# RMSNorm with SiLU on one core: block 0's first row leaves in a transfer of its own

## The chip, the cores and the metric

The kernel runs on one core of a Trainium2 chip. The metric is the device time of one execution in microseconds (us), as the median of several runs. The engines that matter are VectorE (DVE), ScalarE (ACT), which also issues stores to its DMA queue, SyncE (SP), which issues loads to its own, and the core's 16 DMA engines, which carry the packets of both queues. TensorE (PE) is used only at the start.

## What is computed

The input `x` has 8 x 1024 rows of 2048 float32 values, 67.1 MB; the output has the same size. Each row is divided by its root mean square, multiplied by `gamma`, and put through SiLU:

```python
rms = np.sqrt(np.mean(x ** 2, axis=-1, keepdims=True) + eps)
out = gamma * x / rms
return (out * (1 / (1 + np.exp(-out)))).astype(np.float32)
```

## The kernel before

The 8192 rows are cut into 16 blocks of 512. A block is a tile `xt` of 128 partitions; each partition holds J = 4 neighbouring rows, 32 KB that are contiguous in DRAM, so a block is one load of 4 MB (line 52) and, but for the last, one store of 4 MB (line 93). Six buffers hold the blocks. Before anything else one of them serves as `grow`, into which gamma is loaded (line 108); PE copies gamma to all partitions (line 112).

The work of a block `b` has three parts, and all of it happens in place:

- `sums(b)`, lines 58 to 75: the sums of squares. DVE takes rows 2 and 3 (line 64), ACT rows 0 and 1 (line 68, Square with an accumulator); ACT then takes the square root (line 74).
- `invert(b)`, line 79: DVE's reciprocal.
- `finish(b)`, lines 82 to 90: for each of the four rows DVE multiplies by the reciprocal and by gamma (line 84). After rows 1 and 3 ACT applies SiLU to the pair of rows just done (line 88). With `halves`, for the last block alone, the pair is stored at once (line 90).

The order on each engine is the order in which the program is written, since the kernel uses a manual schedule. Loads 0 to 4 are issued at the start, load 5 once `grow` is free. Then block 0 is summed, inverted and finished, block 1 is summed, and from there the loop of lines 124 to 127 runs `sums(b + 1, after_first=[b - 1])`, `finish(b)`, `invert(b + 1)`. The argument `after_first` is where stores are issued: `sums` calls `store(b - 1)` after its first Square (lines 70 to 72), so block 0's store is issued by ACT in the middle of `sums(2)`. `store(b)` also issues load `b + 6` on SP (line 95). That load writes into the buffer that block `b` leaves, so SP waits until the store has landed. The last stores are issued by lines 128, 130 and 90.

The DMA issues of ACT stand in ACT's instruction order, those of SP in SP's. Each transfer is spread over the 16 DMA engines, 8 partitions on each, one packet per partition; a small packet at the end of each engine's share updates a semaphore.

Of the kernel before, what the change touches and what calls it, by code (L numbers as in the profile page):

```python
# [1 line left out]

# [4 lines left out]

ACT = mybir.ActivationFunctionType
ALU = mybir.AluOpType


@with_exitstack
def kernel(
    ctx: ExitStack,
    tc: tile.TileContext,
    x: bass.AP,
    gamma: bass.AP,
    eps: bass.AP,
    out: bass.AP,
):  # L20

    nc = tc.nc
    P = nc.NUM_PARTITIONS
    f32 = mybir.dt.float32
    x2 = x.flatten_outer_dims()
    o2 = out.flatten_outer_dims()  # L30
    n, d = x2.shape
    J = 4
    BUFS, LEAD = 6, 6
    nblk = n // (P * J)
    xb = x2.rearrange("(b p j) d -> b p (j d)", p=P, j=J)
    ob = o2.rearrange("(b p j) d -> b p (j d)", p=P, j=J)

    singles = ctx.enter_context(tc.tile_pool(name="singles", bufs=1))
    pool = ctx.enter_context(tc.tile_pool(name="pool", bufs=BUFS))
    small = ctx.enter_context(tc.tile_pool(name="small", bufs=2))  # L40
    psum = ctx.enter_context(tc.tile_pool(name="psum", bufs=1, space=bass.MemoryType.PSUM))

    g = singles.tile([P, d], f32)
    eps_t = singles.tile([P, 1], f32)
    ones = singles.tile([P, P], f32)
    junk_a = psum.tile([P, d], f32, name="junk_a")
    junk_v = psum.tile([P, d], f32, name="junk_v")
    blocks, rmss, rstds = {}, {}, {}

    def load(b):  # L50
        xt = pool.tile([P, J * d], f32, name="xt")
        nc.sync.dma_start(out=xt, in_=xb[b])  # L52
        blocks[b] = xt

    def row(b, j):
        return blocks[b][:, j * d:(j + 1) * d]

    def sums(b, after_first=()):


        ss = small.tile([P, J], f32, name="ss")
        na = J // 2
        for j in range(na, J):
            nc.vector.tensor_tensor_reduce(  # L64
                out=junk_v, in0=row(b, j), in1=row(b, j), scale=1.0, scalar=0.0,
                op0=ALU.mult, op1=ALU.add, accum_out=ss[:, j:j + 1])
        for j in range(na):
            nc.scalar.activation(out=junk_a, in_=row(b, j), func=ACT.Square,  # L68
                                 accum_out=ss[:, j:j + 1])
            if j == 0:  # L70
                for s in after_first:
                    store(s)
        rms = small.tile([P, J], f32, name="rms")
        nc.scalar.activation(out=rms, in_=ss, func=ACT.Sqrt, scale=1.0 / d, bias=eps_t)  # L74
        rmss[b] = rms

    def invert(b):
        rstd = small.tile([P, J], f32, name="rstd")
        nc.vector.reciprocal(out=rstd, in_=rmss.pop(b))  # L79
        rstds[b] = rstd  # L80

    def finish(b, halves=False):
        for j in range(J):
            nc.vector.scalar_tensor_tensor(out=row(b, j), in0=row(b, j), scalar=rstds[b][:, j:j + 1],  # L84
                                           in1=g, op0=ALU.mult, op1=ALU.mult)
            if j % 2:
                cols = slice((j - 1) * d, (j + 1) * d)
                nc.scalar.activation(out=blocks[b][:, cols], in_=blocks[b][:, cols], func=ACT.Silu)  # L88
                if halves:
                    nc.scalar.dma_start(out=ob[b][:, cols], in_=blocks[b][:, cols])  # L90

    def store(b):
        nc.scalar.dma_start(out=ob[b], in_=blocks[b])  # L93
        if b + LEAD < nblk:
            load(b + LEAD)

    with tc.manual_schedule():


        Q = 4  # L100
        w = d // Q
        grow = pool.tile([P, J * d], f32, name="xt")
        for b in range(BUFS - 1):
            load(b)
        nc.vector.memset(ones, 1.0)  # L105
        nc.vector.memset(eps_t, float(eps))  # L106
        nc.scalar.activation(out=junk_a[:, 0:1], in_=ones[:, 0:1], func=ACT.Square)  # L107
        nc.scalar.dma_start(out=grow[0:P:P // Q, 0:w],
                            in_=bass.AP(tensor=gamma.tensor, offset=gamma.offset, ap=[[w, Q], [1, w]]))
        for c in range(Q):  # L110
            k = c * (P // Q)
            nc.tensor.matmul(junk_v[:, c * w:(c + 1) * w], ones[k:k + 1, :], grow[k:k + 1, 0:w],  # L112
                             start=True, stop=True)
        nc.vector.tensor_copy(out=g, in_=junk_v)  # L114
        load(BUFS - 1)


        last = nblk - 1
        sums(0)
        invert(0)  # L120
        finish(0)
        sums(1)
        invert(1)
        for b in range(1, last - 1):
            sums(b + 1, after_first=[b - 1])
            finish(b)
            invert(b + 1)
        store(last - 2)
        finish(last - 1)
        store(last - 1)  # L130
        sums(last)
        invert(last)
        finish(last, halves=True)


# [1 line left out]
_INS = ['x', 'gamma', 'eps']  # L137
_OUTS = [((8, 1024, 2048), 'float32')]

_NUMBERS = {'eps': 9.999999747378752e-06}  # L140


# [26 lines left out]
```

## Time and profile before

| | us |
|---|---|
| Median of 4 runs (317.46 to 317.84) | 317.72 |
| The profiled execution | 317.7 |
| Its span, from first to last instruction | 315.9 |
| DVE busy | 223.5 (71% of the span) |
| ACT busy | 223.8 (71%) |
| PE busy | 2.1 (1%) |
| One 4 MB load, issue to landing (median of 16) | 41.5 |
| One 4 MB store, issue to landing (median of 15) | 35.8 |
| One 2 MB store of the last block, the same (median of 2) | 10.6 |

The DMA engines moved 134.25 MB, 425 GB/s over the span. "Busy" is time in which an engine executes instructions; DMA issues aren't counted in it. Issue to landing includes the time that a transfer stands in its queue behind others, so a large figure alone doesn't say that the transfer is slow. In the rows of stretches, the columns are: the stretch in us from the start of the span, its length, the busy time of PE, PE's weight load, DVE, ACT and GpSimd with their instruction counts, the granted PE clock, the mean busy share of the 16 DMA engines, and GB/s. A packet is counted where its record lies, so a short stretch can show a share over 1.

### The profile page before, as it was taken

The numbers are of one execution on the slowest core, as the hardware profiler recorded it, in microseconds if no ns is written. First come the engines' busy times: TensorE is split into PE (matmuls) and PEld (weight loads), VectorE is DVE, ScalarE is ACT, GpSimd is POOL, SyncE is SP. The second block draws the span as 40 slices with busy tenths as digits, with TensorE's granted clock in tenths as the row PEclk, the third lists the DMA queues.
The fourth block names the chain that finished last, engine by engine and source line by source line (L and its number), as shares of the span: only waits on it lengthen the run. The fifth ranks groups of instructions, "written<-read, shape, count | busy, mean of one in ns | idle before, by whom it ended". The sixth has DMA issues, their size and how long they took to land.

```text
span 315.9 us, 444 instructions
## 1 busy us (share of the span) xinstructions
PE 2.1 (1%) x8; PEld 0.5 (0%) x8; DVE 223.5 (71%) x147; ACT 223.8 (71%) x144; POOL 0.2 (0%) x4
## 2 busy tenths in 40 slices
PE   0200000000000000000000000000000000000000
PEld 0000000000000000000000000000000000000000
DVE  0679499999494884939759296693957939993900
ACT  1357958999967778668777677676686776889440
POOL 0000000000000000000000000000000000000000
DMA  8999999999999999999999999999999999999996
GB/s 333 402 461 415 448 386 411 456 407 465 398 462 402 457 411 452 419 444 431 431 436 431 444 419 448 415 456 407 461 402 461 407 456 407 456 411 452 427 420 290
DMA packets 4763, 134.25 MB, mean 425 GB/s; under 512 B 532, under 2 KB 532, under 8 KB 536
## 3 DMA queue, kind: packets, MB, share of 16 engines
q1 hardware_dynamic: 2304, 67.11, 49.8%
q10 hardware_dynamic: 2456, 67.12, 49.2%
q14 instruction: 3, 0.02, 0.0%
HBM read 67.12 MB, written 67.11 MB: 425 GB/s over the span
## 4 chain that ended last, share of the span: by engine, by line
DMA 66%; DVE 18%; ACT 8%; issue 4%; DVEq 1%; ACTq 0%; SPq 0%
DMA xt<-in_x_dram 44%; DMA out_dram<-xt 23%; DVE xt L84 13%; ACT xt L88 5%; DVE junk_v L64 4%; ACT junk_a L68 2%; ACT L74 1%; DVEq L164 1%; ACT rms L74 0%; DVE rstd L79 0%; DVE ss L64 0%; ACTq L93 0%; SPq L52 0%; DVEq L64 0%; ACTq L74 0%
## 5 line engine op out<-in xcount | busy, mean ns | idle before, releaser
L84 DVE SCALAR_TENSOR_TENSOR xt<-xt,rstd,g 128x2048 f32<-128x2048 f32 x64 | 146.2, 2348 | 0.1
L88 ACT ACTIVATE xt<-xt 128x4096 f32<-128x4096 f32 x32 | 115.4, 3615 | 36.8 <-DVE xt L84 36.7
L64 DVE CUSTOM_DVE_ANT_0 junk_v<-xt 128x2048 f32<-128x2048 f32 x32 | 73.6, 2298 | 55.5 <-DMA xt<-in_x_dram 54.9
L68 ACT ACTIVATE junk_a<-xt 128x2048 f32<-128x2048 f32 x32 | 60.1, 1879 | 28.6 <-DMA xt<-in_x_dram 27.7
L74 ACT ACT_TABLE_LOAD x15 | 19.2, 1283 | 9.9 <-DVE ss L64 9.9
L88 ACT ACT_TABLE_LOAD x15 | 19.2, 1283 | 3.1 <-DVE xt L84 2.9
L79 DVE RECIPROCAL rstd<-rms 128x4 f32<-128x4 f32 x16 | 2.8, 174 | 11.3 <-ACT rms L74 11.3
L114 DVE COPY g<-junk_v 128x2048 f32<-128x2048 f32 x1 | 2.3, 2292 | 9.3 <-PE junk_v L112 9.3
L68 ACT ACTIVATION_READ_ACCUMULATOR junk_a<-xt 128x1 f32 x32 | 6.0, 186 | 0.0
L74 ACT ACTIVATE rms<-ss,eps_t 128x4 f32<-128x4 f32 x16 | 4.8, 297 | 1.2 <-DVE ss L64 1.1
L64 DVE DVE_READ_ACCUMULATOR2_ANT ss<- 128x1 f32 x32 | 4.5, 142 | 0.0
L112 PE MATMUL junk_v<-xt,ones 1*128 1x512 f32 x8 | 2.1, 1132 | 8.1 <-DMA xt<-in_gamma_dram 8.1
L107 ACT ACT_TABLE_LOAD x1 | 1.3, 1283 | 0.7 <-PEq L150 0.7
L105 DVE MEMSET ones<- 128x128 f32 x1 | 0.2, 165 | 0.8 <-PEq L150 0.8
L112 PEld LDWEIGHTS junk_v<-xt,ones 1*128 1x128 f32 x8 | 0.5, 308 | 8.1 <-issue 8.1
L107 ACT ACTIVATE junk_a<-ones 128x1 f32<-128x1 f32 x1 | 0.2, 174 | 0.0
L150 POOL MEMSET const-uint8-127<- 128x1 uint8 x1 | 0.1, 102 | 0.0
L150 POOL MEMSET const-bfloat16-1.0<- 128x1 bf16 x1 | 0.1, 101 | 0.0
L150 POOL MEMSET const-float32-0.0<- 128x1 f32 x1 | 0.1, 98 | 0.2 <-issue 0.2
L150 POOL MEMSET const-float32-1.0<- 128x1 f32 x1 | 0.1, 98 | 0.0
L106 DVE MEMSET eps_t<- 128x1 f32 x1 | 0.1, 59 | 0.0
## 6 DMA issues: line engine op xcount, KB each, us to landing
xt<-in_x_dram SPq DMA_DIRECT2D x16, 4096.0 KB, 41.5
out_dram<-xt ACTq DMA_DIRECT2D x15, 4096.0 KB, 35.8
out_dram<-xt ACTq DMA_DIRECT2D x2, 2048.0 KB, 10.6
xt<-in_gamma_dram ACTq DMA_DIRECT2D x1, 8.0 KB
```

Of the source, the lines that this page charges most:

```text
L64: nc.vector.tensor_tensor_reduce(out=junk_v, in0=row(b, j), in1=row(b, j), scale=1.0, scalar=0.0, op0=ALU.mult, op1=ALU.add, accum_out=ss[ ...
L68: nc.scalar.activation(out=junk_a, in_=row(b, j), func=ACT.Square, accum_out=ss[:, j:j + 1])
L74: nc.scalar.activation(out=rms, in_=ss, func=ACT.Sqrt, scale=1.0 / d, bias=eps_t)
L79: nc.vector.reciprocal(out=rstd, in_=rmss.pop(b))
L84: nc.vector.scalar_tensor_tensor(out=row(b, j), in0=row(b, j), scalar=rstds[b][:, j:j + 1], in1=g, op0=ALU.mult, op1=ALU.mult)
L88: nc.scalar.activation(out=blocks[b][:, cols], in_=blocks[b][:, cols], func=ACT.Silu)
L105: nc.vector.memset(ones, 1.0)
L107: nc.scalar.activation(out=junk_a[:, 0:1], in_=ones[:, 0:1], func=ACT.Square)
L112: nc.tensor.matmul(junk_v[:, c * w:(c + 1) * w], ones[k:k + 1, :], grow[k:k + 1, 0:w], start=True, stop=True)
L114: nc.vector.tensor_copy(out=g, in_=junk_v)
L150: nc = _bacc.Bacc("TRN2", target_bir_lowering=False, num_devices=1)
L164: with _tile.TileContext(nc) as tc:
```

## The change

Block 0's store is cut in two. In `finish(0)`, right after the SiLU of rows 0 and 1, ACT issues a store of row 0 alone: 8 KB in each partition, 1 MB. The other three rows, 24 KB in each partition, 3 MB, are stored where the whole block was stored, after the first Square of `sums(2)`. Row 1 is done when row 0 is, but goes with the later transfer. Load 6, which takes block 0's buffer, is issued at the same place in SP's order. All other blocks are stored as they were.

```diff
             if j == 0:
                 for s in after_first:
-                    store(s)
+                    store(s, slice(0 if s else 1, J))
...
-    def finish(b, halves=False):
+    def finish(b, halves=False, first_row=False):
...
                 nc.scalar.activation(out=blocks[b][:, cols], in_=blocks[b][:, cols], func=ACT.Silu)
+                if first_row and j == 1:
+                    nc.scalar.dma_start(out=ob[b][:, 0:d], in_=row(b, 0))
                 if halves:
                     nc.scalar.dma_start(out=ob[b][:, cols], in_=blocks[b][:, cols])
 
-    def store(b):
-        nc.scalar.dma_start(out=ob[b], in_=blocks[b])
+    def store(b, rows=slice(0, J)):
+        c = slice(rows.start * d, rows.stop * d)
+        nc.scalar.dma_start(out=ob[b][:, c], in_=blocks[b][:, c])
         if b + LEAD < nblk:
             load(b + LEAD)
...
-        finish(0)
+        finish(0, first_row=True)
```

## The prediction

> **What bounds the kernel now.** I read the page's slices and queues first, then the DMA rate in stretches, the chain that ended last, and the timeline around the edit. The page's slices and queue rows:
>
> ```profile
> DMA  8999999999999999999999999999999999999996
> GB/s 333 402 461 415 448 386 411 456 407 465 398 462 402 457 411 452 419 444 431 431 436 431 444 419 448 415 456 407 461 402 461 407 456 407 456 411 452 427 420 290
> q1 hardware_dynamic: 2304, 67.11, 49.8%
> q10 hardware_dynamic: 2456, 67.12, 49.2%
> ```
>
> All slices but the two end ones have the 16 DMA engines at 90% or more, and the packets of loads (q1) and stores (q10) together fill 99.0% of 16 engines' span. DVE and ACT are busy 71% each. The rate by stretch (last column GB/s; the column before it is the DMA share):
>
> ```profile
> 6.00:34.00 28.00, 2.09 (x8) 0.55 (x8) 20.96 (x14) 15.38 (x10) 0.00 (x0) 1.00 1.00 433
> 36.00:48.00 12.00, 0.00 (x0) 0.00 (x0) 9.68 (x8) 8.04 (x11) 0.00 (x0) 1.00 1.00 393
> 84.00:258.00 174.00, 0.00 (x0) 0.00 (x0) 124.21 (x81) 126.80 (x81) 0.00 (x0) 1.00 1.00 433
> 278.00:312.00 34.00, 0.00 (x0) 0.00 (x0) 17.38 (x11) 20.28 (x11) 0.00 (x0) 1.00 1.00 431
> ```
>
> Loads alone (6 to 34 us) ran at 433, loads and stores mixed (84 to 258) at 433, stores alone (278 to 312) at 431. So it doesn't matter for the rate which direction moves; only bytes, and moments in which an engine has no packet, count. The one stretch that falls short is 36 to 48, where the first store joins the loads; I come back to it. The packet records say the same from the other side: a 32 KB packet took 1.213 us on its engine whether load or store, and each engine had a packet in hand from 1.7 us to between 313.0 and 314.6 us. The last semaphore update of a store came at 314.99, and the span ends at 315.9. The chain that ended last agrees as far as it goes:
>
> ```profile
> DMA 66%; DVE 18%; ACT 8%; issue 4%; DVEq 1%; ACTq 0%; SPq 0%
> ```
>
> The DVE and ACT shares in it are instructions beside which the engines had queued packets all the time, so they aren't time that can be taken out. **The end is the sum of the packets**, as long as nothing lets a queue run dry.
>
> **The change, part by part.** The timeline around the edit (start, length, engine; the brackets give idle time before):
>
> ```profile
> 24.58 3.62 ACT L88 ACTIVATE xt<-xt 128x4096 f32<-128x4096 f32 x1 [3.60 <-DVE xt L84]
> ...
> 29.11 3.62 ACT L88 ACTIVATE xt<-xt 128x4096 f32<-128x4096 f32 x1 [0.91 <-DVE xt L84]
> ...
> 36.69 0.36 ACTq L93 DMA_DIRECT2D out_dram<-xt  x1
> ```
>
> *ACT's queue.* One more DMA issue stands between the two Silus of block 0. The first ends at 28.20, the second starts at 29.11, since it waits 0.91 us for DVE. An issue at L93 or L90 took 0.34 to 0.36 us, so it lies wholly in that wait: 0. Without that cover it would put ACT back 0.36 us once, and the DMA queues would hide it. The issue waits only for ACT's own Silu; queued behind it is the second Silu, which isn't due yet.
>
> *SP's queue.* Load 6 goes into block 0's buffer, so it now waits for two stores. One more wait of this kind takes 0.03 us on SP. What counts is when the second store lands (below).
>
> *Packets.* Block 0's store was 8 packets of 32 KB on each engine. It becomes 8 of 8 KB and 8 of 24 KB. The records have 0.084 us for 2 KB (gamma), 0.611 for 16 KB (the halves of the last block) and 1.213 for 32 KB. Between 2 and 16 KB that is 0.0376 us per KB, so 8 KB costs 0.310 and 24 KB, midway between 16 and 32, costs 0.912. Together 1.222 against 1.213: 8 x 0.009 = 0.07 us, and a further semaphore packet at 0.009: **+0.08 us**.
>
> *The join.* When store 0 joined, the load packets between 38.7 and 42.5 us took up to 2.25 us in place of 1.213; their excess sums to 1.02 us per engine (in the rate: 393 against 433 over 12 us is 1.1 us). No later store shows it, since each arrives while an earlier one is still in the queue. The change moves the join 8.5 us ahead and starts it with 8 KB packets. No row shows a join with small packets, so I bound it: 0 if it goes with packet size (a gain of 1.02), 2.04 if the second transfer has to join as well (a loss of 1.02). I take 1.02, unchanged, the one row there is; the first store then still fills the queue when the second comes: 8 small packets alternate with 8 loads, 8 x (0.310 + 1.213) = 12.2 us, and join at about 32.2 (28.2 plus the 3.9 us that the first packets of store 0 took from issue), so they last to 44, while the rest is issued at 36.69.
>
> *Who gets data later.* From about 32 us on, loads share with stores. Load 3's landing had come at 45.3; the load before it landed at 32.6, so it is now due by 32.6 + 12.2 + 1.0 = 45.8. DVE reaches it at 52.16. Load 4 alternates with the 24 KB packets: 8 x (1.213 + 0.912) = 17.0 us, so 62.8 in place of 64.7; DVE reaches it at 65.89. Neither is missed. Store 0 had landed 24.5 us after its issue at 36.69, of which 8 x 2 x 1.213 = 19.4 are packets. The pair needs 8 x (1.213 + 0.310) + 8 x (1.213 + 0.912) = 29.2, so it lands at 28.2 + 5.1 + 29.2 = 62.5, against 61.2. Load 6 is issued 1.3 us later, but load 5 fills the load queue until about 84. Store 1, issued at 55.84 by ACT, still comes before store 0's packets run out.
>
> ```profile
> 55.84 0.34 ACTq L93 DMA_DIRECT2D out_dram<-xt  x1
> ...
> 84.05 1.88 ACT L68 ACTIVATE junk_a<-xt 128x2048 f32<-128x2048 f32 x1 [0.30 <-DMA xt<-in_x_dram]
> ```
>
> From 84.05 on, compute waits for loads. Loads have then got ahead by about half a packet per engine, so this comes a microsecond or so earlier, and the same bytes are left for the end as stores. An early arrival of data there buys nothing: the last half-block was issued at 304.22, while the engines worked on the half before it until 308.9 or later. That is 4.7 us of margin in either direction.
>
> *Sum:* 0 + 0 + 0.08 + 0 (join) = +0.1. The profiled execution took 317.7 with a span of 315.9, so **317.8**; the median of four was 317.72, which gives the same.
>
> The Trainium skill speaks against such a split. "DMA: Bandwidth & Descriptors" (Anatomy of one DMA — SWDGE (gpsimd) path; Rules for kernel authors) gives each DMA some 2.0 us of fixed cost on that path and advises to coalesce. By it the sum would be about 319.8, an estimate from that page. This case's row disagrees for queued transfers: the last two stores, 16 KB packets each, landed at 310.15 and 314.99, 4.84 us apart, and 8 x 0.611 = 4.89 are packets alone, so there's no room for a fixed cost.
>
> **Rivals.**
>
> *Small packets are dear, slower.* In the records, code fetches of 8 KB took 0.307 to 0.493 us, most 0.474 before the program's start. Were the 128 row packets (8 KB in every 32 KB of the output) to cost 0.474 to 0.493, that adds 8 x 0.165 to 8 x 0.183 = 1.3 to 1.5 us: 319.1 to 319.3. It decides from 0.39 us a packet on (0.64 us / 8 above 0.310). For it: no store packet of 8 KB is in the trace. Against it: 2 KB at 0.084 and 16 KB at 0.611 are on the line, and the three 8 KB fetches during the run took 0.309. A second join, +1.02 to 318.8, would lie in the same direction.
>
> *The join gets cheaper, faster.* If the 1.02 us belongs to the first 32 KB packets, small ones pay a quarter, or nothing: 317.8 - 1.02 = 316.8. For it: it is the largest loss of DMA time between 10 and 313 us. Against it: the first loads at 1.7 us show a like delay (0.70 us per engine), which looks like a start-up latency that no size changes.
>
> *The edit does nothing to the end*, since stores are hidden behind the queues anyway: this is the forecast. One doubt lies within it. The engines end between 313.0 and 314.6, and three 8 KB code fetches ("q14 instruction: 3" on the page) fall on single engines; the longest two load packets after 50 us follow two of them, so another place of a fetch can move the end by about 0.5 us. Own range 317.3 to 318.4.
>
> **How the numbers follow.** About 0.2% (0.64 us) is what a measurement of this kernel can tell from no change. Forecast (within it): 0.68. Small packets dear or a second join (slower): 0.19. Join cheaper, or a luckier end of the slowest engine (faster): 0.13. The range takes in the cheap join and the dear packets' lower price: 316.7 to 319.1.
>
> **What would show it.** Right: a store issue of 1 MB at about 28.2; 8 KB packets at 0.31 us and 144 more packets on q10; load 6 issued at 62 to 63; rates of 430 and more after the join; one short stretch of about 1 us per engine, now near 32; the last two stores issued earlier than or at 299.69 and 304.22, and the end unmoved. Wrong: 8 KB packets well over 0.31, a second short stretch near 40, a slice in the middle under 9 tenths, or no short stretch at all. If some queue runs dry because compute waits on a late load, my claim that only the packets' sum counts is wrong.

## The result and the profile after

The changed kernel has a median of 320.42 us over 34 runs, from 317.34 to 327.36; the kernel before has 317.65 over 56 runs, from 317.22 to 318.41. The ratio of the times is 1.0033, with a 95% interval of 1.0020 to 1.0046. That ratio counts only runs within 1.5% of the same kernel's fastest; 13 of the 34 runs of the changed kernel lie above that, at 322.25 to 327.36, and no run of the kernel before does, so the spread belongs to the change and is part of the result. With all runs the medians stand at 320.42 / 317.65 = 1.0087.

So the change costs 0.33% by that ratio, and more with all runs counted. The forecast was 317.8 and no change beyond 0.2%. By the ratio the changed kernel takes 317.65 x 1.0033 = 318.7 us, inside the stated range of 316.7 to 319.1 but 0.9 above the forecast; the median of all runs, 320.42, lies above the range.

The profiled execution took 320.58 us with a span of 318.8, against 317.7 and 315.9 before. These are the page's slices and queue rows of the changed kernel:

```profile
DMA  8999999999999999999999999999999999999994
GB/s 330 428 428 421 427 411 422 436 444 423 399 420 411 445 428 428 432 428 444 428 436 436 424 444 419 448 428 432 432 428 444 432 436 432 428 440 419 445 415 197
...
q10 hardware_dynamic: 2600, 67.12, 49.3%
q1 hardware_dynamic: 2304, 67.11, 49.2%
```

No slice in the middle is under 9 tenths, so the DMA engines are as busy as before. What has grown is the time of the same bytes. Stores (q10) fill 49.3% of 318.8 = 157.2 us per engine, against 49.2% of 315.9 = 155.4 before; loads (q1) 156.8 against 157.3. The 144 added packets are there (2600 against 2456), but the packet records price them at 0.08 us. Only the last slice has thinned out, from 6 tenths to 4. The stretches, with GB/s last, show where:

```profile
6.00:34.00 28.00, 2.09 (x8) 0.54 (x8) 20.96 (x14) 15.37 (x10) 0.00 (x0) 1.00 1.01 433
36.00:48.00 12.00, 0.00 (x0) 0.00 (x0) 9.67 (x8) 8.04 (x11) 0.00 (x0) 1.00 1.00 415
84.00:258.00 174.00, 0.00 (x0) 0.00 (x0) 123.02 (x81) 126.44 (x81) 0.00 (x0) 1.00 1.00 431
278.00:312.00 34.00, 0.00 (x0) 0.00 (x0) 18.77 (x12) 21.33 (x11) 0.00 (x0) 1.00 1.00 430
...
82.00:102.00 20.00, 0.00 (x0) 0.00 (x0) 13.80 (x9) 15.74 (x10) 0.00 (x0) 1.00 1.01 418
...
312.00:314.00 2.00, 0.00 (x0) 0.00 (x0) 0.00 (x0) 0.00 (x0) 0.00 (x0) 1.00 0.69 295
314.00:316.00 2.00, 0.00 (x0) 0.00 (x0) 0.00 (x0) 0.00 (x0) 0.00 (x0) 1.00 0.38 164
316.00:318.00 2.00, 0.00 (x0) 0.00 (x0) 0.00 (x0) 0.00 (x0) 0.00 (x0) 1.00 0.15 66
```

The stretch of the join (36 to 48) has become better, 415 against 393. The stretch from 82 to 102 has become worse, 418 against the 444 of the kernel before (part of that is how packets fall into the stretch: at the shares beside them, 1.01 and 1.03, a busy engine's rate is 414 against 431):

```profile
82.00:102.00 20.00, 0.00 (x0) 0.00 (x0) 13.80 (x9) 15.85 (x10) 0.00 (x0) 1.00 1.03 444
```

And the end is ragged: from 312 to 318 the DMA share falls from 0.69 to 0.15, because some engines are done at about 313 and others only at 317.5. Before, all 16 were done between 313.4 and 314.6, and no packet of data starts from 314 on:

```profile
314.00:316.00 2.00, 0.00 (x0) 0.00 (x0) 0.00 (x0) 0.00 (x0) 0.00 (x0) 1.00 0.00 0
```

The chain that ended last has more of DMA in it, 74% against 66%:

```profile
DMA 74%; DVE 14%; ACT 5%; issue 2%; DVEq 1%; ACTq 0%; SPq 0%
```

The edit's own steps are where they were expected. In the timeline the new issue stands in ACT's wait, and the second SiLU starts at 29.11 as before; compute first waits for a late load at 82.82, a little sooner than the 84.05 of before:

```profile
24.59 3.62 ACT L88 ACTIVATE xt<-xt 128x4096 f32<-128x4096 f32 x1 [3.59 <-DVE xt L84]
28.23 0.35 ACTq L90 DMA_DIRECT2D out_dram<-xt  x1
...
29.11 3.62 ACT L88 ACTIVATE xt<-xt 128x4096 f32<-128x4096 f32 x1 [0.91 <-DVE xt L84]
...
36.70 0.34 ACTq L96 DMA_DIRECT2D out_dram<-xt  x1
...
82.82 2.30 DVE L64 CUSTOM_DVE_ANT_0 junk_v<-xt 128x2048 f32<-128x2048 f32 x1 [3.13 <-DMA xt<-in_x_dram]
```

**What the packets show.** Each packet record has a start, a length, a queue and a size, but not its engine. A packet starts within a few ns of the end of the one before it on the same engine, so the engines can be strung together from that (where several end within a few ns, two strings can be swapped). Below is the order on two engines of each kernel. L is a load packet of 32 KB, S a store packet of 32 KB, `a` one of 8 KB, `r` one of 24 KB; "." and "," are the small semaphore packets that end an engine's share of a load and of a store.

```
before:  LLLLLLLLS.SLSLSLSLSLSLSL,LS.SLSLSLSLSLSLSL,LS.S    first S at 42.3
before:  LLLLLLLSLS.SLSLSLSLSLSL,LSLS.SLSLSLSLSLSL,LSLS.    first S at 40.7
after:   LLLLLLLLa.aLaLaLaLaLaLaL,Lr.rLrLrLrLrLrLrL,LS.S    first a at 31.8 to 32.2, 8 engines
after:   LLLLLLLL.LaLaLaLaLaLaLaLa.,LrLrLrLrLrLrLrLr.,LS    first a at 32.8 to 33.6, 8 engines
```

Loads and stores take turns, so where the first store packet falls fixes how store blocks stand to load blocks for the rest of the run. Before the change it falls ahead of the "." that ends load 3, nearly everywhere with one or two store packets before it. After the change it meets the end of load 2. On 8 engines it comes just ahead of that ".", on the other 8 one load packet behind it; these then run in step, "." and "," together.

From 46 us on, 139 store packets last over 1.23 us, and each of them is on one of the 8 engines in step. On one of those, four consecutive store packets from 69.98 us on took 1.594, 1.527, 1.549 and 1.441 us; on the engines ahead each took 1.213. Their excess over 1.213 us goes from 69.8 us to about 127, sums to 1.46 us per engine over all 16, and to some 3 to 4 us on the five worst, the ones that end at 317.1 to 317.5. Before the change the same sum is 0.02. The join itself cost 0.66 us per engine, against 1.02.

### The profile page after: what moved, and what is told of

Same layout as the page of the kernel before. It is cut to its first block, busy times and chain, and to the rows that moved or that the text cites. A ratio compares the mean times of both kernels' runs of the same rounds, so it can differ in the third digit from the quotient of the medians.

```text
span 318.8 us, 447 instructions
## 1 busy us (share of the span) xinstructions
PE 2.1 (1%) x8; PEld 0.5 (0%) x8; DVE 223.5 (70%) x147; ACT 223.6 (70%) x144; POOL 0.2 (0%) x4
## 3 DMA queue, kind: packets, MB, share of 16 engines
q10 hardware_dynamic: 2600, 67.12, 49.3%
q1 hardware_dynamic: 2304, 67.11, 49.2%
## 4 chain that ended last, share of the span: by engine, by line
DMA 74%; DVE 14%; ACT 5%; issue 2%; DVEq 1%; ACTq 0%; SPq 0%
DMA xt<-in_x_dram 41%; DMA out_dram<-xt 33%; DVE xt L84 11%; ACT xt L88 3%; DVE junk_v L64 3%; ACT junk_a L68 1%; DVEq L168 1%; ACT L74 0%; ACT rms L74 0%; DVE rstd L79 0%; ACTq L96 0%; DVE ss L64 0%; SPq L52 0%; DVEq L64 0%; ACTq L74 0%
```

## Experiments

The theory that these were made for: the change costs time because its first store packet meets the end of a load, so that engines fall into different orders. The rivals: the cut costs by itself (small packets), or the early start does. "Ahead by n" below says that n store packets of the engine stand before the "." of the load that was ending, "behind by n" that n load packets stand between it and the first store packet; all of it is read from the packet records of one profiled execution each.

### 1. The cut alone, at the usual place

```diff
                 for s in after_first:
+                    if s == 0:
+                        nc.scalar.dma_start(out=ob[0][:, 0:d], in_=row(0, 0))
                     store(s, slice(0 if s else 1, J))
...
-                if first_row and j == 1:
-                    nc.scalar.dma_start(out=ob[b][:, 0:d], in_=row(b, 0))
```

> Block 0's store is cut into 8 KB and 24 KB per partition as in the changed kernel, but both are issued at the usual place, in the middle of the next sums. Phase theory (the changed kernel loses time because the first store packet of some DMA engines falls just behind the semaphore packet of a load block, so that these engines run load blocks and store blocks in step, and there store packets take 1.2 to 1.65 us instead of 1.213): the first packets come at about 40.6 to 42.6 us as before the change, ahead of that semaphore packet, so every run is within 0.5 us of 317.7 and no store packet after 46 us is long. Rival, small packets (the cut itself costs): the spread of the changed kernel, 317.3 to 327 with a median near 320, comes back.

Measured: 317.76 (317.29 to 318.06, 11 runs), ratio 1.0001 (0.9992 to 1.0009). Both parts were issued at 36.66 and 37.05, all engines were ahead, and the 8 KB and 24 KB packets took 0.309 and 0.912 us. **The cut costs nothing**; the rival of small packets is out.

### 2. A pair of rows early

```diff
-                    store(s, slice(0 if s else 1, J))
+                    store(s, slice(0 if s else 2, J))
...
-                    nc.scalar.dma_start(out=ob[b][:, 0:d], in_=row(b, 0))
+                    nc.scalar.dma_start(out=ob[b][:, 0:2 * d], in_=blocks[b][:, 0:2 * d])
```

> Rows 0 and 1 (16 KB per partition) go early at 28.2 us, rows 2 and 3 follow at the usual place. Phase theory: the first store packets fall at 31.8 to 33.6 us, on both sides of the semaphore packet of load 2, as in the changed kernel, so the times spread again, 317.3 to 325 or so, median above 319, and the engines that start behind that packet are the ones with long store packets. Rival, small packets of 8 KB: with 16 KB none is small, so 317.7 within 0.5.

Measured: 318.04 (317.44 to 321.48, 11 runs), ratio 1.0033 (1.0009 to 1.0056). The spread is there, without an 8 KB packet, but smaller than expected: the median stays under 319. The profiled execution took 317.87, with 7 engines ahead and 9 behind, and 86 store packets over 1.23 us; their excess was 0.52 us per engine. All but one of the 86 were on seven of the nine engines behind, as expected. So engines in both orders don't cost the same each time.

### 3. Row 0 written behind the second SiLU

```diff
-                if first_row and j == 1:
+                if first_row and j == 3:
```

> Row 0 still goes early and alone, but after the second SiLU, at about 32.7 us, so that the first packets come at 36 to 38 us, in the middle of load 3 and not at its border. Phase theory: load and store blocks are some four packets out of step on all engines, no long store packets, 317.7 within 0.5 in every run. Rival, early start (sharing with stores before the usual place costs by itself): a median of 319 or more and a spread, since 4 of the 8.5 us remain.

Measured: 317.99 (317.28 to 321.95, 12 runs), ratio 1.0029 (1.0005 to 1.0054). It wasn't the experiment that was meant. The issue needs only row 0, and ACT's queue reached it as the second SiLU began:

```profile
29.01 3.62 ACT L88 ACTIVATE xt<-xt 128x4096 f32<-128x4096 f32 x1 [0.91 <-DVE xt L84]
29.02 0.35 ACTq L90 DMA_DIRECT2D out_dram<-xt  x1
```

So the packets came 0.8 us later than in the changed kernel, and all 16 engines were behind the end of load 2, 14 of them by one packet. With all in step the excess of store packets was small, 0.18 us per engine in an execution of 318.35. Being in step is not dear by itself.

### 4. The whole store, one Square later

```diff
-            if j == 0:
+            if j == (1 if 0 in after_first else 0):
                 for s in after_first:
```

> No cut: block 0 is stored whole as before the change, but issued one Square later, at about 38 us in place of 36.69. Phase theory: the first packets come 1 to 2 us later, so on most engines behind the semaphore packet of load 3 (which lies at about 42.5); these run in step, store packets of 1.3 to 1.6 us appear, and the times spread above 319 without any cut. Rival, the cut or the early start is what costs: 317.7 within 0.5, as before the change.

Measured: 321.91 (321.61 to 322.28, 4 runs), ratio 1.0137 (1.0122 to 1.0152). **With no cut and no early start, a later issue costs about 4 us in each of the four runs.** The issue came at 40.12, later than meant, and the first packets two or three behind the end of load 3 on all engines. The loss has another form than in the changed kernel, seen in the queue rows:

```profile
q1 hardware_dynamic: 2304, 67.11, 49.9%
q10 hardware_dynamic: 2456, 67.12, 48.7%
```

Of a span of 319.9, loads take 159.6 us per engine, against 157.3 before the change; stores 155.8 against 155.4. Here it's load packets that are long, 199 of them after 46 us, all through the run: 427 GB/s from 84 to 258 us. They lie where one store transfer ends and the next begins: by the strings some 140 of the 199 are the first or second load packet behind the "," of a store.

```profile
84.00:258.00 174.00, 0.00 (x0) 0.00 (x0) 120.84 (x79) 126.38 (x81) 0.00 (x0) 1.00 1.00 427
```

The expectation named store packets and a spread; it had neither. Only the place of the join as a cause is confirmed.

### 5. The changed kernel again

> The changed kernel once more, for a second profile. Phase theory: the time goes with how the engines split at the first store packet. If its time is above 319, some engines start behind the semaphore packet of load 2 while others start ahead of it, and the long store packets lie on the former; if it is near 317.5, hardly any store packet after 46 us is over 1.23 us. Rival (the engines' order has nothing to do with it): long store packets lie on engines of both kinds.

Measured: 321.99 in one run, and the profile is of that run. Nine engines were ahead and seven behind; 182 store packets of 32 KB were long, with an excess of 2.24 us per engine. In the strings all but one of them lie on the seven engines behind, as the theory expected; a few strings can be swapped in this record, so the match isn't certain for three engines. These are stretches of it:

```profile
82.00:102.00 20.00, 0.00 (x0) 0.00 (x0) 13.80 (x9) 15.63 (x10) 0.00 (x0) 1.00 1.00 415
...
318.00:320.00 2.00, 0.00 (x0) 0.00 (x0) 0.00 (x0) 0.00 (x0) 0.00 (x0) 1.00 0.10 41
```

The same short rate as in the first profile and a still later end go with the larger excess.

### 6. and 7. Other blocks side by side

Both kernels take the blocks in the order 0, 8, 1, 9, ...; number 6 is the changed kernel with that, number 7 the whole store issued one Square late.

```diff
+    at = [b // 2 + (nblk // 2) * (b % 2) for b in range(nblk)]
...
-        nc.sync.dma_start(out=xt, in_=xb[b])
+        nc.sync.dma_start(out=xt, in_=xb[at[b]])
...
-        nc.scalar.dma_start(out=ob[b][:, c], in_=blocks[b][:, c])
+        nc.scalar.dma_start(out=ob[at[b]][:, c], in_=blocks[b][:, c])
```

> The changed kernel, with the blocks of input and output taken in the order 0, 8, 1, 9, ... and nothing else moved, so that a load and a store that run side by side are 8 MB apart in their tensors and not 16 MB. The times of issue, the packets and the engines' split stay as they are. If the loss is a matter of addresses in DRAM (in-step engines read and write places that collide), it changes: a median well below 320, near 317.7, or well above. If it is a matter of the engines' order alone, the spread of 317.3 to 327 with a median near 320 comes back.

Measured: 318.15 (317.35 to 329.75, 12 runs), ratio 1.0019 (1.0000 to 1.0039).

> The uncut store issued one Square later, which took 321.9, with the blocks in the order 0, 8, 1, 9, ... Addresses: the 4 us go or change by more than 1 us. Order of the engines' packets alone: 321.5 to 322.5 again.

Measured: 321.86 (320.68 to 322.52, 4 runs), ratio 1.0128 (1.0111 to 1.0145). The late store's loss doesn't care which blocks lie side by side. For the changed kernel the spread came back, wider even, with a lower median; 12 runs against 34 of a time that varies so much don't tell whether it is less. The profiled execution of number 6 (317.54) had 5 engines ahead and 11 behind and an excess of only 0.11 us per engine: once more both orders at once, without the loss.

### 8. The first load in halves

```diff
-        nc.sync.dma_start(out=xt, in_=xb[b])
+        if b == 0:
+            for c in (slice(2 * d, 4 * d), slice(0, 2 * d)):
+                nc.sync.dma_start(out=xt[:, c], in_=xb[b][:, c])
+        else:
+            nc.sync.dma_start(out=xt, in_=xb[b])
```

> The changed kernel with load 0 cut in two, rows 2 and 3 ahead of rows 0 and 1, so that block 0's sums end about 0.8 us sooner and row 0's store is issued near 27.4 us. The loads keep their borders. Phase theory: the first store packet then comes ahead of the semaphore packet of load 2 on all or nearly all engines, as it does ahead of that of load 3 before the change; no long store packets, every run within 0.6 of 317.5. Rival, sharing early costs by itself: the spread stays, median above 319.

Measured: a median of 317.57 (317.19 to 332.79, 11 runs), ratio 0.9996 (0.9987 to 1.0006). Row 0 went at 27.10. In the profiled execution (317.19) all 16 engines were ahead, and the excess of store packets was 0.05 us per engine. But three of the 11 runs took 324.87, 326.97 and 332.79. The first packets came at 31.9 to 32.3 us, right at the end of load 2, so 1 us sooner wasn't clear of it. What the engines did in those three runs no profile shows.

### 9. Row 0 clear of the border: earlier still, cut as in the change

```diff
+            if first_row and j == 0:
+                nc.scalar.activation(out=row(b, 0), in_=row(b, 0), func=ACT.Silu)
+                nc.scalar.dma_start(out=ob[b][:, 0:d], in_=row(b, 0))
             if j % 2:
-                cols = slice((j - 1) * d, (j + 1) * d)
+                cols = slice((j if first_row and j == 1 else j - 1) * d, (j + 1) * d)
...
-                if first_row and j == 1:
-                    nc.scalar.dma_start(out=ob[b][:, 0:d], in_=row(b, 0))
```

> Row 0 gets a SiLU of its own and is stored right behind it, at about 24.3 us; row 1 gets its own SiLU later, the rest goes at the usual place. The first store packets then come near 28 us, some three packets ahead of the semaphore packet of load 2 on every engine. Theory of the join (ahead of a load's semaphore packet on all engines is good, astride or behind is bad): no engine runs in step, few or no long store packets, every run within 0.6 of 317.4. Rival, an early and cut store costs by itself: earlier is worse, median above 320.

Measured: 317.40 (317.29 to 318.11, 11 runs), ratio 0.9998 (0.9990 to 1.0007). The timeline has the issue 4 us ahead of that of the changed kernel, and the first packets came at 28.0 to 29.9, ahead of the end of load 2 by three to four on every engine:

```profile
22.33 1.91 ACT L87 ACTIVATE xt<-xt 128x2048 f32<-128x2048 f32 x1 [1.33 <-DVE xt L84]
24.27 0.35 ACTq L88 DMA_DIRECT2D out_dram<-xt  x1
```

```profile
84.00:258.00 174.00, 0.00 (x0) 0.00 (x0) 124.19 (x81) 126.74 (x81) 0.00 (x0) 1.00 1.00 434
```

The excess of store packets after 46 us is 0.04 us per engine, and from 84 to 258 the rate is 434. **Starting still earlier, with the same cut of the store, removes the loss**, so neither the cut nor the early start is its cause.

### 10. Row 0 in the next block's sums

```diff
+            if b == 1 and j == 0:
+                nc.scalar.dma_start(out=ob[0][:, 0:d], in_=row(0, 0))
             if j == 0:
                 for s in after_first:
...
-                if first_row and j == 1:
-                    nc.scalar.dma_start(out=ob[b][:, 0:d], in_=row(b, 0))
```

> Row 0 is stored after the first Square of block 1, near 32.7 us, first packets at 36.3 to 38 us, in the middle of load 3, four packets behind the semaphore packet of load 2 and four ahead of that of load 3. Theory of the join: neither astride nor just behind, so 317.7 within 0.6 in nearly every run. Rival, any lag behind the load's semaphore packet costs as in the uncut store that went one Square late: 320 to 322 in every run.

Measured: 318.12 (317.33 to 318.92, 11 runs), ratio 1.0019 (1.0008 to 1.0030). ACT's queue ran ahead of its engine again: the issue came at 28.94, though the Square ahead of it in the program ran at 32.46.

```profile
28.94 0.35 ACTq L71 DMA_DIRECT2D out_dram<-xt  x1
...
32.46 1.86 ACT L68 ACTIVATE junk_a<-xt 128x2048 f32<-128x2048 f32 x1
```

So it repeats number 3 and isn't the middle of a load; the nearest to that are numbers 9 and 11, where five or six of a load's eight packets had gone. All 16 engines were one packet behind, in step. The spread is 1.6 us where the changed kernel has 10, and the excess of store packets 0.17 us per engine. Together with number 3: with all engines behind by about one packet the cost is some 0.2 to 0.3%; among the kernels that join at the end of load 2, the large losses come where the two orders can be mixed.

### 11. The whole store, 2 us sooner

```diff
-            if j == 0:
+            if b == 1 and j == 1:
+                store(0)
+            if j == 0 and b != 2:
                 for s in after_first:
```

> No cut: block 0 is stored whole 2 us sooner than before the change, behind the second Square of block 1, near 34.7 us, first packets at 38.3 to 40 us, two to three packets ahead of the semaphore packet of load 3. Theory of the join: all ahead, so 317.6 within 0.5 in every run. Rival, a store that starts before the usual place costs by itself: above 318.5.

Measured: 317.42 (317.22 to 317.74, 11 runs), ratio 0.9996 (0.9987 to 1.0004). The issue came at 34.53, the first packets at 38.4 to 39.9, ahead of the end of load 3 by three to four on all engines. No gain and no loss: a store that joins well ahead of the border is free.

### 12. The whole store behind a tiny instruction

```diff
                 for s in after_first:
+                    if s == 0:
+                        nc.scalar.activation(out=junk_a[:, 0:1], in_=ones[:, 0:1], func=ACT.Square)
                     store(s)
```

> No cut and no early store: block 0 is stored whole at the usual place, with one tiny Square of one column ahead of the issue, which delays it from 36.69 to about 38 us and costs ACT 0.2 us that no queue sees. The first packets then fall around the semaphore packet of load 3, at 42 to 44 us. Theory of the join: some or all engines start just behind that packet, run in step, long store packets appear, and the times spread from 317.5 to 322 or more, median above 318.5. Rival, it takes a cut or an early store: 317.7 within 0.5 in every run.

Measured: 321.93 (321.14 to 322.49, 4 runs), ratio 1.0136 (1.0116 to 1.0156). The delay was larger than meant. In the kernel before, the issue had left ACT's queue ahead of the Square; behind the tiny instruction it left only as that ran, at 40.01:

```profile
40.00 0.17 ACT L73 ACTIVATE junk_a<-ones 128x1 f32<-128x1 f32 x1
40.01 0.36 ACTq L95 DMA_DIRECT2D out_dram<-xt  x1
```

The first packets fell two to three behind the end of load 3, as in number 4, and the same loss came, again in load packets (3.53 us per engine after 46 us, stores 0.11). It says that a 0.17 us instruction on ACT can cost 4 us of the run; a whole store that meets the border exactly wasn't tried.

### The runs side by side

| Kernel | Issue (us) | First store packets to the load's end | Median (range) |
|---|---|---|---|
| 9, cut | 24.27 | ahead by 3 to 4 | 317.40 (317.29 to 318.11) |
| 11, whole | 34.53 | ahead by 3 to 4 | 317.42 (317.22 to 317.74) |
| before, whole | 36.69 | ahead, nearly all by 1 to 2 | 317.65 (317.22 to 318.41) |
| 1, cut | 36.66 | ahead by 1 to 2 | 317.76 (317.29 to 318.06) |
| 8, cut | 27.10 | ahead by 1, at the border | 317.57 (317.19 to 332.79) |
| the change | 28.23 | 8 ahead by 1, 8 behind by 1 | 320.42 (317.34 to 327.36) |
| 6, cut, blocks in the order 0, 8, ... | 28.20 | 5 ahead by 1, 11 behind by 1 | 318.15 (317.35 to 329.75) |
| 2, cut in halves | 28.09 | 7 ahead by 1, 9 behind by 1 | 318.04 (317.44 to 321.48) |
| 10, cut | 28.94 | behind by 1 | 318.12 (317.33 to 318.92) |
| 3, cut | 29.02 | behind by 1 to 2 | 317.99 (317.28 to 321.95) |
| 12, whole | 40.01 | behind by 2 to 3 | 321.93 (321.14 to 322.49) |
| 4, whole | 40.12 | behind by 2 to 3 | 321.91 (321.61 to 322.28) |
| 7, whole, blocks in the order 0, 8, ... | 40.08 | behind by 2 to 3 | 321.86 (320.68 to 322.52) |

Cut and whole kernels stand on both sides of the loss, early and late ones too. In the third column, the kernels with all engines ahead have no loss in their profiles, though number 8, right at the end, has three runs from 324.87 up; those with engines behind are all slower in the median. The column doesn't give the size of the loss, since engines on both sides of the end cost 0.4 us in the median of number 2 and 2.8 in that of the change. It is also a circle: each engine carries eight packets of a load, so "ahead by 3 to 4" in numbers 9 and 11 is five to six load packets behind the end of the load before. The loss was seen at the end itself and at one to three load packets behind it; four wasn't tried.

## Where the prediction held and where it failed

**What held.** The steps that were worked out from rows came out within a few tenths. The issue stood at 28.23 (28.2) and cost ACT nothing. The small packets took 0.309 and 0.912 us (0.310, 0.912). Load 3 landed at 45.82 (by 45.8), load 4 at 63.08 (62.8), the pair of stores at 62.68 (62.5), and load 6 was issued at 62.7 (62 to 63). One sign of being right failed: the last two stores were issued at 301.1 and 305.6, not at or before 299.69 and 304.22. The Trainium skill's page "DMA: Bandwidth & Descriptors" (Anatomy of one DMA — SWDGE (gpsimd) path) gives a fixed cost of some 2.0 us per DMA for DMAs that GpSimd issues. The stores here are issued by ACT, and no such cost is seen for one that is queued: in experiment 1 the extra DMA moved the time by a ratio of 1.0001 (0.9992 to 1.0009).

**The number came near by luck.** 318.7 lies inside 316.7 to 319.1 only because the range was drawn up to the price of small packets, and experiment 1 shows no such price. What made the kernel slower was in none of the terms.

**The step that failed** is the first: "So it doesn't matter for the rate which direction moves; only bytes, and moments in which an engine has no packet, count", and with it "The end is the sum of the packets". No queue ran dry, and the sum of the packets did set the end. But the length of a packet was taken as 1.213 us from the trace of before, and that holds only for the order of packets that this trace has. With some engines in step, store packets took up to 1.66 us (1.90 in the second profile); the slowest engine set the end at 317.5 in place of 314.6. (The first engine of before ends at 313.4, not at 313.0 as the text has it; nothing rests on that.) The loss is +2.9 us of span where the sum had +0.1.

**The join.** The bounds were 0 to 2.04 us with 1.02 taken. It cost 0.66 in the changed kernel, in two parts, 0.20 near 29 to 33 us and 0.46 at 42 to 45, so the second stretch that was named as a sign of error is there. It comes as the 24 KB packets take over from the 8 KB ones, though the queue of stores hadn't run empty; the text had argued that this would spare the second transfer. Experiment 1 has such a second part too (0.3 us at 51 to 54), and experiment 2, whose parts are equal, has none. The rival of a cheaper join was right about that, at -0.36 us, but the time went elsewhere. What the join decides for the rest of the run, the order, was in no rival: the text moved it by 8.5 us and asked only what it costs by itself, not which load's end it would meet. The rows for that question were at hand, since the first packets at about 32.2 and load 2's landing at 32.6 both stand in its text.

**The rivals.** "Small packets are dear" had the right sign and a price near the result (319.1 to 319.3 against 317.65 x 1.0033 = 318.7), but experiment 1 shows that its mechanism is not at work. The spread of 10 us was foreseen nowhere.

**What stays open.** Whether there is a loss goes with the place of the first store packets against the load's end; moving the issue either way by a few microseconds, with and without the cut, showed it. Why a store packet takes longer on an engine in step, while others aren't, is not settled: experiments 2 and 6 have both orders at once in executions of 317.87 and 317.54. Both profiles of an early, cut store with a large loss have the mixture, but these two show that it is not sufficient. Nor is it known why load packets, not store packets, are long when the stores join two or three packets behind. The distance between the blocks that are read and written at the same time makes no difference for the latter (experiment 7). Collisions of reads and writes in DRAM that depend on the moment would be one explanation; no run here shows them. The experiments ran on three chips: 1 to 4 on one, 5 to 8 on the second, 9 to 12 on the third. The kernel before took 317.66, 317.62 and 317.47 there, and the late whole store 321.91, 321.86 and 321.93, so the chips agree on both. But the changed kernel was run again only on the second, once, so its own spread on the other two isn't shown; numbers 2, 3 and 10, which join at the same load's end, were slower there.

## What to carry to other kernels

In a kernel that DMA bounds from end to end, a moved transfer costs or gains nothing in bytes, but it can change the order in which loads and stores take turns on each engine, and that order lasts. Ask where the first packet of a moved store falls among the packets of the other queue, and keep it a few packets clear of the end of a transfer: 3 to 4 packets ahead gave medians of 317.4 and no run over 318.2 here, the border itself 317 to 333, 2 to 3 behind 321.9. Look at the range of the times as well as at their median, since one profile shows only one of the orders.

## What was not expected of the hardware

- The length of a 32 KB packet isn't a constant of the engine: 1.213 us in most rows, up to 1.9 us for stores, and up to 2.25 us for loads when the other queue joins (1.99 at the borders of experiment 4).
- An engine that falls behind isn't helped by the others: in the strings each engine carries eight packets of every 4 MB load and store, whatever its delay. In the changed kernel the engines' ends lay 4 us apart, and the DMA share in the last stretches fell to 0.15.
- ACT's queue can issue a DMA well before instructions that stand ahead of it in the program have run: 28.94 us against 32.46 for the Square ahead of it in experiment 10. Behind one more instruction the same queue issued only at 40.01 in place of 36.69.
